# Split values in layer 1, later reads, loads and stores: one edit of a two-layer backbone kernel

## The chip, the core and the metric

The kernel runs on one core of one Trainium2 chip. The metric is the device time of one launch in microseconds (us). The engines are TensorE (PE; its weight loads are listed apart as PEld), VectorE (DVE), ScalarE (ACT), GpSimd (POOL) and SyncE (SP), which here only issues DMAs.

## What is computed

```python
for i in range(2):                                    # two layers; tokens 256 context + 1024 latent, D = 1024
    mod = silu(c) @ w_ada[i] + b_ada[i]               # six modulation vectors, for latent and for context
    h = modulate(rmsnorm(x, g_pre), sh1, sc1)
    p = h @ w_in[i]                                   # q (8 heads of 64), k, v (2 heads), u (512 columns)
    out = softmax(window and context scores, sink) @ v    # blocks of 128 queries, 3 + 2 blocks of keys
    four = fourier_mix(u, w_fourier[i])
    x_mid = x + g1 * rmsnorm(concat(out, four) @ w_out[i], g_post)
    hf = modulate(rmsnorm(x_mid, g_preffn), sh2, sc2)
    x = x_mid + g2 * rmsnorm((silu(hf @ w_gate[i]) * (hf @ w_up[i])) @ w_down[i], g_postffn)
    ...                                               # layer 0 does the same for the context tokens
```

Inputs and output are 32-bit. The large products are made of three cheaper ones each: an operand is split into a high part and the rest ("hi", "lo"), and hi·hi, lo·hi and hi·lo are added up in PSUM.

## The kernel before

The 1280 tokens lie in `X` (SBUF, features on partitions) in two blocks of 640 columns; in layer 1 the latent tokens alone, 512 and 512. A layer runs through these stages: input projection (`inproj`), attention (`attn`) with the rest of the projection, the Fourier mixing and the first block's output projection as filling work (`fill`), the second output projection, the FFN's up part (`ffn_up`, f16 products from sums of quarter matrices) and its down part (`ffn_down`).

**Order.** Stages are generators, and `mix` takes the next step from the one that has done the smallest share of its length; a scheduler then orders each engine's instructions by a model of their times. Each engine then runs its own list in that order, and so does SP: a DMA that has to wait, for a buffer or for its source, holds all DMAs behind it.

**Attention.** `Pair` (a class) does one unit: 128 queries, two heads. `score` makes the scores and their exponentials; `turn` transposes two key tiles of 128 (four transposes, L227) into a PSUM tile `tp` and ACT copies it to SBUF (`PT`, a ring of six, L231); `value` multiplies them by `V`. A unit has 5 key tiles, in the first and last query block 4, so 3 turns or 2; there are 32 units in layer 1. `value` packs: the product of an even key tile writes PSUM partitions 0 to 63, that of an odd one 64 to 127, both plain 32-bit (L244), and `finish` adds the halves. The score products are of another 32-bit type, `fp32r`; the profile shows both as f32.

**PSUM.** `ps` is a ring of four tiles that `tp`, `pv`, the narrow projections (`accn`), the Fourier products and the modulation share.

**Weights.** `weight` (L398 to L402) loads a 512 KB tile into `raw` (a ring of four), ACT casts it to hi, DVE makes lo. `ada` (L541, L570) makes layer 0's modulation with loads in the same ring, one load ahead of its products throughout the attention. `ahead` and `sums` make the weights of four FFN pairs early and store hi (ACT's queue, L471) and lo (SP's queue, L472) in DRAM.

**FFN down.** `hidden` issues the reads of hidden values that went to DRAM (L1198): 3 tiles of block 0, then all 11 of block 1, two reads each. `ffn_down` loads each w_down row in three pieces (L1211), scales them by hidden-tile factors (ACT L1216, DVE L1217) and multiplies (L1224).

**Between the layers.** The second block's post-norm (`postnorm`, L786 adds the residual) runs beside layer 1's first projections; with `share=True` every other add goes to POOL. Then `xstats` (squares, a sum by TensorE at L669 into `nps`, some DVE steps) and `spread` (L691, `rps`) give the norm that `scaled` (L714) uses.

```python
            mix((fill, FILL[l]), (self.attn(l, queries), ATT[l]), (work, 17), (early, 8 * AHEAD))
...
        for blk in range(2):
            for f in range(KEPT if blk == 0 else 0, NP):
                for e in range(2):
                    self.nc.sync.dma_start(places[blk][f][e], self.hs[blk, f, e, :, 0:w2])
```

## Time and profile before

| | us |
|---|---|
| median of three runs | 2496.72 (2495.13 to 2501.28) |
| the profiled execution | 2501.49 |
| its span, first to last instruction | 2499.7 |
| PE, DVE, ACT, POOL busy | 2377.2, 1658.1, 1347.8, 201.2 |
| mean granted clock of TensorE | 0.982 of full speed |

Busy time is counted per engine, and engines overlap, so it does not add up to the span. TensorE is busy for 95% of it; a granted clock below 1 means that it ran part of the time at 1.2 GHz in place of 2.4.

### The profile page before, as it was taken

The numbers are of one execution on the slowest core, as the hardware profiler recorded it, in microseconds if no ns is written. First come the engines' busy times: TensorE is split into PE (matmuls) and PEld (weight loads), VectorE is DVE, ScalarE is ACT, GpSimd is POOL, SyncE is SP. The second block draws the span as 40 slices with busy tenths as digits, with TensorE's granted clock in tenths as the row PEclk, the third lists the DMA queues.
The fourth block names the chain that finished last, engine by engine and source line by source line (L and its number), as shares of the span: only waits on it lengthen the run. The fifth ranks groups of instructions, "written<-read, shape, count | busy, mean of one in ns | idle before, by whom it ended". The sixth has DMA issues, their size and how long they took to land. (4 is left out here: it accounts for less than half of the span.)

```text
span 2499.7 us, 43891 instructions
## 1 busy us (share of the span) xinstructions
PE 2377.2 (95%) x17212; PEld 1856.0 (74%) x17212; DVE 1658.1 (66%) x3338; ACT 1347.8 (54%) x2587; POOL 201.2 (8%) x204
## 2 busy tenths in 40 slices
PE   7989989999999999998999989999989999999997
PEld 4877777797776666665777877877778888884586
DVE  5457676567837887777864595574677567765485
ACT  4476566657534455544654355576674456545473
POOL 0313110010000000000000043210100000000000
PEclk9999989999999999999999989999999999999998
DMA  8535423567654334559774231101496512237474
GB/s 303 188 112 176 154 94 119 195 226 280 209 180 139 124 129 161 159 193 365 271 246 145 94 119 39 35 18 51 172 341 221 169 60 85 77 107 243 131 251 130
DMA packets 157376, 406.83 MB, mean 163 GB/s; under 512 B 17488, under 2 KB 34288, under 8 KB 157168
## 3 DMA queue, kind: packets, MB, share of 16 engines
q1 hardware_dynamic: 147952, 389.33, 46.4%
q10 hardware_dynamic: 9216, 14.68, 1.6%
q8 instruction: 135, 2.21, 0.3%
q14 instruction: 73, 0.60, 0.1%
HBM read 339.19 MB, written 64.76 MB: 162 GB/s over the span
## 5 line engine op out<-in xcount | busy, mean ns | idle before, releaser
L1086 PE MATMUL p<-ffn,ww 128*128 128x320 f16 (+1 forms) x7392 | 923.4, 287 | 29.0 <-ACT ww L466 7.7
L1086 PEld LDWEIGHTS <-ww 128*128 128x128 f16 x7392 | 723.2, 98 | 226.1 <-issue 25.9
L1224 PEld LDWEIGHTS <-wd 128*128 128x128 f16 x3696 | 362.3, 98 | 167.1 <-ACT wd L1216 10.4
L1224 PE MATMUL acc<-hid,wd 128*128 128x320 f16 (+2 forms) x2544 | 335.7, 294 | 9.4 <-ACT wd L1216 9.1
L520 PE MATMUL accn<-arena,hi 128*128 128x320 f32 (+1 forms) x992 | 266.8, 336 | 4.6 <-ACT arena L231 2.3
L1217 DVE SCALAR_TENSOR_TENSOR wd<-raw,dn,wd 128x256 f16<-128x256 f32 x440 | 186.3, 481 | 126.2 <-ACT wd L1216 126.1
L1216 ACT ACTIVATE wd<-raw,dn 128x256 f16<-128x256 f32 x440 | 186.6, 496 | 134.7 <-PE acc L1224 78.1
L520 PE MATMUL acc<-arena,hi 128*128 128x320 f32 (+2 forms) x928 | 211.7, 333 | 3.5 <-ACT X L1040 2.5
L520 PEld LDWEIGHTS accn<-arena,hi 128*128 128x128 f32 x992 | 175.4, 191 | 25.7 <-issue 11.4
L1224 PE MATMUL acc<-X,wd 128*128 128x320 f16 (+1 forms) x1152 | 190.3, 326 | 0.7 <-ACT wd L1216 0.4
L520 PEld LDWEIGHTS acc<-arena,hi 128*128 128x128 f32 x928 | 156.7, 192 | 21.9 <-issue 4.6
L520 PE MATMUL accn<-arena,lo 128*128 128x320 f32 (+1 forms) x496 | 160.2, 326 | 0.0
L676 POOL TENSOR_TENSOR nr<-nm,mhalf 128x5 f32<-128x5 f32 (+2 forms) x17 | 19.9, 1169 | 1707.0 <-DVE nm L675 1670.9
L402 DVE TENSOR_TENSOR lo<-raw,hi 128x1024 fp32r<-128x1024 f32 x77 | 100.7, 1308 | 77.4 <-ACT hi L401 53.5
L216 DVE TENSOR_REDUCE ng<-score 128x1 f32<-128x641 f32 (+2 forms) x144 | 107.3, 747 | 63.6 <-PE score L209 62.0
L466 ACT ACTIVATE ww<-raw,sp 128x1024 f16<-128x1024 f32 x112 | 110.0, 1033 | 65.0 <-DVE raw L481 47.4
L231 ACT COPY arena<-tp 128x512 f32<-128x512 f32 (+1 forms) x184 | 96.7, 530 | 85.9 <-PE tp L227 84.2
L467 DVE SCALAR_TENSOR_TENSOR ww<-raw,sp,ww 128x1024 f16<-128x1024 f32 x112 | 125.8, 1147 | 25.0 <-ACT ww L466 24.8
L217 ACT ACTIVATE A<-score,ng 128x641 f32<-128x641 f32 (+2 forms) x144 | 106.5, 740 | 46.4 <-DVE ng L216 32.5
L401 ACT CAST hi<-raw 128x1024 fp32r<-128x1024 f32 x77 | 80.6, 1047 | 87.9 <-PE acc L520 37.1
L520 PE MATMUL acc<-arena,lo 128*128 128x320 f32 (+2 forms) x464 | 125.3, 329 | 0.0
L244 PE MATMUL pv<-arena 128*64 128x256 f32 x640 | 116.0, 407 | 2.5 <-ACT arena L231 2.5
(228 smaller groups left out, 3448.8 us busy)
## 6 DMA issues: line engine op xcount, KB each, us to landing
raw<-in_wdown SPq DMA_DIRECT2D x112, 512.0 KB, 4.8
ww<-wc SPq DMA_DIRECT2D x96, 512.0 KB, 4.5
raw<-in_wgate SPq DMA_DIRECT2D x60, 512.0 KB, 4.6
raw<-in_wup SPq DMA_DIRECT2D x60, 512.0 KB, 4.4
wm<-in_wada SPq DMA_DIRECT2D x96, 256.0 KB, 4.4
raw<-in_wdown SPq DMA_DIRECT2D x56, 384.0 KB, 4.6
raw<-in_win SPq DMA_DIRECT2D x40, 512.0 KB, 3.6
wada<-in_wada SPq DMA_DIRECT2D x39, 512.0 KB, 4.4
```

Of the source, the lines that this page charges most:

```text
L216: nc.vector.tensor_reduce(self.ng[:, hs], sv, axis=AX.X, op=ALU.max, negate=True)
L217: nc.scalar.activation(p, sv, AF.Exp, bias=self.ng[:, hs], accum_out=self.su[:, hs])
L231: nc.scalar.copy(pt, tp[:, 0:256 * n])
L244: nc.tensor.matmul(self.pv[HD * i:HD * i + HD, 0:256], net.V[:, self.kts[k], self.g, :], pt[:, 256 * i:256 * i + 256], start=(j == 0), sto ...
L402: nc.vector.tensor_tensor(lo[:, 0:w], raw[:, 0:w], hi[:, 0:w].bitcast(F32), op=ALU.subtract)
L466: nc.scalar.activation(hi, src, AF.Copy, scale=s)
L467: nc.vector.scalar_tensor_tensor(lo, src, s, hi, op0=ALU.mult, op1=ALU.subtract)
L520: self.nc.tensor.matmul(ps, wt[:, ks], xt[:, a:b], start=(k == 0 and i == 0), stop=(k == n - 1 and i == 2))
L1086: nc.tensor.matmul(ps, w[:, at:at + P], G[k // 2][:, k % 2, x, c, 0:h], start=(start and k + t == 0), stop=(k == KD // 2 - 1 and t == 2), ...
L1216: nc.scalar.activation(wt[:, 0, c], raw[:, c], AF.Copy, scale=r)
L1217: nc.vector.scalar_tensor_tensor(wt[:, 1, c], raw[:, c], r, wt[:, 0, c], op0=ALU.mult, op1=ALU.subtract)
L1224: nc.tensor.matmul(out, wt[:, e, k], xs[x][:, s, u:v], start=(f + s + i == 0), stop=(f == NP - 1 and s == 1 and i == 2))
```

## The change

In layer 1 (`whole` is false) `V` and the transposed exponentials are kept as hi and lo in `fp32r`; a value product is now 128 columns wide (V's hi beside its lo) and done twice, with the exponentials' hi and lo, for each key tile. DVE makes the lo parts. Two ring places serve one turn, so the six hold three turns. Layer 0 keeps the plain form.

Block 1's hidden reads become a third generator, `rest`, beside the first down products. A lo store of a made weight is issued at the next step of its generator and behind the latest load. `ada` has no standing load ahead: a unit loads its four tiles shortly before its products, then pauses for 1.7 steps; it no longer runs beside the first projection. Between the layers DVE does all residual adds, and the norm's steps are paced 8 to that projection, not 10.

```diff
@@ Pair.turn
-        pt = net.PT[net.npt % len(net.PT)][:, 0:256 * n]
-        net.npt += 1
+        parts = 1 if net.whole else 2
+        pt = [net.PT[(net.npt + e) % len(net.PT)][:, 0:256 * n] for e in range(parts)]
+        net.npt += parts
         with net.tc.high_priority(offset=AHEAD_OF):
-            nc.scalar.copy(pt, tp[:, 0:256 * n])
+            nc.scalar.copy(pt[0], tp[:, 0:256 * n])
+            if parts > 1:
+                nc.vector.tensor_tensor(pt[1], tp[:, 0:256 * n], pt[0].bitcast(F32), op=ALU.subtract)
@@ Pair.value
-            nc.tensor.matmul(self.pv[HD * i:HD * i + HD, 0:256], net.V[:, self.kts[k], self.g, :], pt[:, 256 * i:256 * i + 256],
-                             start=(j == 0), stop=(k + 2 >= len(self.kts)))
+            v, c = net.V[:, self.kts[k], self.g, :], slice(256 * i, 256 * i + 256)
+            if net.whole:
...
+            else:
+                for e in range(2):
+                    nc.tensor.matmul(self.pv[:, 0:256], v, pt[e][:, c], start=(k + e == 0), stop=(k == len(self.kts) - 1 and e == 1))
@@ sums
             if keep:
-                to = self.copy(l, i, j, self.WIDE[j])
-                nc.scalar.dma_start(to[:, 0], hi)
-                nc.sync.dma_start(to[:, 1], lo)
+                nc.scalar.dma_start(self.copy(l, i, j, self.WIDE[j])[:, 0], hi)
+                made.append((j, lo))
...
+        def store():
+            for j, lo in made:
+                with self.tc.issue_after(self.loaded.ins):
+                    nc.sync.dma_start(self.copy(l, i, j, self.WIDE[j])[:, 1], lo)
+            made.clear()
@@ ada
+            if not raws:
+                load()
+                yield 0.15
             for q in range(4):
-                load()
+                if ahead or q < 3:
+                    load()
...
-                yield 0.5
+                yield 0.5 if ahead else 0.15
...
-            yield 0.5
+            yield rest
@@ evac (values)
-                nc.scalar.copy(self.V[:, a // P + i0:a // P + i0 + n], src)
+                v = self.V[:, a // P + i0:a // P + i0 + n]
+                nc.scalar.copy(v[:, :, :, 0:HD], src)
+                if not self.whole:
+                    nc.vector.tensor_tensor(v[:, :, :, HD:P], src, v[:, :, :, 0:HD].bitcast(F32), op=ALU.subtract)
@@ hidden
+        def rest():
+            for f in range(NP):
+                read(1, f)
+                yield
+        for f in range(KEPT, NP):
+            read(0, f)
+        return places, rest()
@@ program
-        work = self.ada(0, range(4, 12), (1,), [])
-        next(work)
+        work = self.ada(0, range(4, 12), (), [], 1.7)
...
-                mix((self.inproj(l, 0, (3, 4, 5)), cost(3, KD, BW)), (side, 10), (part(work, 2), 1))
+                mix((self.inproj(l, 0, (3, 4, 5)), cost(3, KD, BW)), (side, 10))
             else:
-                mix((self.inproj(l, 0, (1, 0, 2, 3, 4, 5)), cost(6, KD, BW - C)), (side, 10))
+                mix((self.inproj(l, 0, (1, 0, 2, 3, 4, 5)), cost(6, KD, BW - C)), (side, 8))
...
-            mix((fill, FILL[l]), (self.attn(l, queries), ATT[l]), (work, 17), (early, 8 * AHEAD))
+            mix((fill, FILL[l]), (self.attn(l, queries), ATT[l]), (work, 20), (early, 8 * AHEAD))
...
-                mix(down(0, 0, w, first), (part(pre, 4 * AHEAD), 4 * AHEAD), (side, 32))
+                mix(down(0, 0, w, first), (part(pre, 4 * AHEAD), 4 * AHEAD), (side, 32), (rest, 14))
...
-                first, side = self.postnorm(l, 1, a1, b1, done, share=True), self.xstats(*B, "B")
+                first, side = self.postnorm(l, 1, a1, b1, done), self.xstats(*B, "B")
```

**The SP queue where layer 0's down products begin**, before, from the second piece of w_down on (`hid` are reads of hidden values, `wc` stores of lo, `raw<-in_wdown` pieces of w_down):

```order
298 L1211 DMA raw<-in_wdown 128x1024
299 L1198 DMA hid_11317<-hs 128x1280 x6
300 L1198 DMA hid_11318<-hs 128x1280 x4
301 L1137 DMA hs<-hid 128x1280 x2
302 L1198 DMA hid_11319<-hs 128x1280 x6
303 L1198 DMA hid_11317<-hs 128x1280
304 L1198 DMA hid_11319<-hs 128x1280
305 L1198 DMA hid_11317<-hs 128x1280
306 L1198 DMA hid_11319<-hs 128x1280
307 L1198 DMA hid_11320<-hs 128x1280 x6
308 L472 DMA wc<-wa 128x1024
309 L472 DMA wc<-wa 128x512
```

The third and fourth pieces follow as rows 310 and 311. The same stretch of the change:

```order
279 L1248 DMA raw<-in_wdown 128x1024
280 L1228 DMA hid_11318<-hs 128x1280 x6
281 L1228 DMA hid_11319<-hs 128x1280 x4
282 L1167 DMA hs<-hid 128x1280 x2
283 L1228 DMA hid_11320<-hs 128x1280 x6
284 L1228 DMA hid_11318<-hs 128x1280
285 L1228 DMA hid_11320<-hs 128x1280
286 L1228 DMA hid_11318<-hs 128x1280
287 L1248 DMA raw<-in_wdown 128x768
288 L1228 DMA hid_11320<-hs 128x1280
289 L1228 DMA hid_11321<-hs 128x1280 x2
290 L482 DMA wc<-wa 128x1024
```

The third piece moved ahead of seven reads and two stores; the fourth is row 293, behind one more store and three more reads.

**TensorE's list where layer 1 begins**, before (`acc` are products of the projection, `nps` and `rps` the norm's sum and spread); the transposes of the values stand 24 products ahead of `nps`:

```order
13829 L520 MATMUL acc<-arena_14484,lo 128x384
13830 L520 MATMUL acc<-arena_14484,hi 128x384
13831 L669 MATMUL nps<-cst,ssq 128x1 x5
13832 L691 MATMUL rps<-cst,nr 128x128 x5
13833 L520 MATMUL acc<-arena_14483,hi 128x384
```

In the change those transposes stand 34 products ahead of `nps` (row 13856), and these rows follow it:

```order
13857 L543 MATMUL acc<-arena_14484,lo 128x384
13858 L543 MATMUL acc<-arena_14484,hi 128x384
13859 L543 MATMUL acc<-arena_14485,hi 128x384
13860 L543 MATMUL acc<-arena_14485,lo 128x384
13861 L543 MATMUL acc<-arena_14485,hi 128x384 x2
13862 L543 MATMUL acc<-arena_14485,lo 128x384
13863 L543 MATMUL acc<-arena_14485,hi 128x384 x2
13864 L543 MATMUL acc<-arena_14485,lo 128x384
13865 L543 MATMUL acc<-arena_14485,hi 128x384 x2
13866 L543 MATMUL acc<-arena_14485,lo 128x384
13867 L543 MATMUL acc<-arena_14485,hi 128x384
13868 L718 MATMUL rps<-cst,nr 128x128 x5
```

So 24 products of 384 columns moved from behind `rps` to places ahead of it, 10 of them ahead of `nps`.

**A unit's value products on TensorE in layer 1**, before, all five key tiles of one unit together:

```order
14918 L209 LDWEIGHTS bf_101
14919 L209 MATMUL score<-sink,bf_101 128x1
14920 L244 MATMUL pv<-arena_14518 64x256 x5
14921 L252 MATMUL pv<-cst,pvl 128x128
14922 L227 MATMUL tp<-cst,A 128x128 x4
```

and in the change (L254; `PTX` is the sixth ring place, a tile of its own):

```order
15005 L254 MATMUL pv<-arena_14519 128x256
15006 L254 MATMUL pv<-PTX,arena_14519 128x256
15007 L254 MATMUL pv<-arena_14519 128x256
15008 L254 MATMUL pv<-PTX,arena_14519 128x256
15009 L254 MATMUL pv<-arena_14519 128x256 x5
15010 L227 MATMUL tp<-cst,A 128x128 x4
15011 L254 MATMUL pv<-arena_14519 128x256
15012 L261 MATMUL pv<-cst,pvl 128x128
```

Five products of 64 columns became ten of 128.

## Rows read from the trace of the kernel before

**Rows 1.** The page, busy us, share of the span, instructions.
```profile
PE 2377.2 (95%) x17212; PEld 1856.0 (74%) x17212; DVE 1658.1 (66%) x3338; ACT 1347.8 (54%) x2587; POOL 201.2 (8%) x204
```

**Rows 2.** Busy us by stretch: stretch, length, each engine, granted clock, DMA share, GB/s.
```profile
200.00:300.00 100.00, 99.02 (x677) 80.44 (x674) 73.14 (x139) 59.88 (x120) 28.51 (x30) 1.00 0.52 172
300.00:360.00 60.00, 51.47 (x338) 40.44 (x338) 42.75 (x90) 35.03 (x73) 12.22 (x14) 0.86 0.34 119
...
1440.00:1480.00 40.00, 28.51 (x153) 27.87 (x152) 35.04 (x49) 15.23 (x23) 15.36 (x13) 0.83 0.36 117
1500.00:1780.00 280.00, 275.71 (x1840) 216.88 (x1839) 157.62 (x354) 169.85 (x382) 51.95 (x60) 1.00 0.12 40
1640.00:1700.00 60.00, 58.12 (x430) 47.33 (x429) 43.90 (x106) 40.56 (x94) 9.71 (x14) 1.00 0.06 19
```

**Rows 3.** Timeline of PE in layer 1's attention: start, us, instruction.
```profile
1603.34 0.28 PE L202 MATMUL score<-arena,qs 128*128 128x256 f32 x1
1603.46 0.28 PE L203 MATMUL score<-arena,qs 128*128 128x256 f32 x1
...
1604.40 0.31 PE L520 MATMUL accn<-arena,lo 128*128 128x320 f32 x1
1604.55 0.31 PE L520 MATMUL accn<-arena,hi 128*128 128x320 f32 x1
1604.79 0.65 PE L244 MATMUL pv<-arena 128*64 128x256 f32 x4
1605.37 0.45 PE L200 MATMUL score<-arena,qs 128*128 128x384 f32 x1
...
1606.73 1.08 PE L244 MATMUL pv<-arena 128*64 128x256 f32 x6
```

**Rows 4.** Line 244, stretch 1400 to 1800: ns min/median/max, first and last start.
```profile
L244 PE MATMUL pv<-arena x304: 379/379/431, 1508.2 to 1772.3; 128*64 128x256 f32 x152
```

**Rows 5.** Line 912: VectorE's subtraction with one operand in PSUM.
```profile
L912 DVE TENSOR_TENSOR arena<-v,arena x16: 664/683/693, 316.2 to 1661.7; 128x512 fp32r<-128x512 f32 x16
```

**Rows 6.** Timeline of SP, PE and ACT where layer 0's down products begin.
```profile
1111.82 14.62 SPq L1198 DMA_DIRECT2D hid<-hs  x16
1126.54 2.25 SPq L472 DMA_DIRECT2D wc<-wa  x2
1129.12 1.16 SPq L1211 DMA_DIRECT2D raw<-in_wdown  x2
...
1135.03 1.30 ACT L1216 ACTIVATE wd<-raw,dn 128x256 f16<-128x256 f32 x3 [10.30 <-DMA raw<-in_wdown]
...
1135.59 7.96 PE L1224 MATMUL acc<-hid,wd 128*128 128x320 f16 x36 [9.06 <-ACT wd L1216]
```

**Rows 7.** Waits of PE, stretch 1440 to 1480: total us, times, longest.
```profile
PE rps L691 <- DVE nr L681: 5.2, 1, 5.2
PE vps L834 <- ACT vt L829: 3.8, 1, 3.8
PE nps L669 <- DVE ssq L663: 2.4, 1, 2.4
```

**Rows 8.** Timeline of DVE and POOL between the layers.
```profile
1431.34 10.42 DVE L714 SCALAR_TENSOR_TENSOR X<-X,scl,r 128x640 f32<-128x640 f32 x8
1435.37 2.00 POOL L786 TENSOR_TENSOR X<-res,X 128x640 f32<-128x640 f32 x1 [0.91 <-ACT ssq L659]
1466.26 6.46 DVE L714 SCALAR_TENSOR_TENSOR X<-X,scl,r 128x640 f32<-128x640 f32 x8 [2.21 <-ACT r L693]
```

**Rows 9.** Timeline of ACT and PE in layer 0's attention.
```profile
313.32 1.04 ACT L401 CAST hi<-raw 128x1024 fp32r<-128x1024 f32 x1 [2.59 <-DMA raw<-in_tabs]
317.28 0.69 PE L227 MATMUL tp<-cst,A 128*128 128x128 f32 x2 [3.77 <-ACT arena L231]
```

**Rows 10.** Waits of the SP queue, stretch 95 to 420: total us, times, longest.
```profile
SPq L472 <- DVE wa L467: 43.4, 13, 8.4
SPq L541 <- PE ada L570: 34.8, 6, 16.2
```

More of the change, by code (lines that the diff above doesn't have):

```diff
@@ L243, in value @@
             k = 2 * j + i
-            nc.tensor.matmul(self.pv[HD * i:HD * i + HD, 0:256], net.V[:, self.kts[k], self.g, :], pt[:, 256 * i:256 * i + 256],
-                             start=(j == 0), stop=(k + 2 >= len(self.kts)))
+            v, c = net.V[:, self.kts[k], self.g, :], slice(256 * i, 256 * i + 256)
+            if net.whole:
+                nc.tensor.matmul(self.pv[HD * i:HD * i + HD, 0:256], v, pt[0][:, c], start=(j == 0), stop=(k + 2 >= len(self.kts)))
+            else:
+                for e in range(2):
+                    nc.tensor.matmul(self.pv[:, 0:256], v, pt[e][:, c], start=(k + e == 0), stop=(k == len(self.kts) - 1 and e == 1))
     def finish(self):
@@ L271, in __init__ @@
         self.A = one.tile([P, 8 * BW + 4], F32, name="A")
+        self.PTX = one.tile([P, 512], F32R, name="PTX")
         self.turn_to(0)
@@ L346, in turn_to @@
     def turn_to(self, l):
-        self.H, (g, v) = self.arena[l % 2], self.new_arena(1 - l % 2, F32)
+        self.whole = l == 0
+        self.H, (g, v) = self.arena[l % 2], self.new_arena(1 - l % 2, F32 if self.whole else F32R)
         self.KHI = [g[:, T * i:T * i + T] for i in range(2)]
         self.KLO = [g[:, 2 * T + T * i:2 * T + T * i + T] for i in range(2)]
-        self.V = v[:, 0:T].rearrange("p (t g d) -> p t g d", g=2, d=HD)
-        self.PT = [v[:, T + 512 * i:T + 512 * i + 512] for i in range(6)]
+        n = T if self.whole else 2 * T
+        self.V = v[:, 0:n].rearrange("p (t g d) -> p t g d", t=T // P, g=2)
+        self.PT = [v[:, n + 512 * i:n + 512 * i + 512] for i in range(6 if self.whole else 5)]
+        if not self.whole:
+            self.PT.append(self.PTX[:])
     def halves(self, i, shape, types, name):
@@ L397, in weight @@
         raw = self.raw.tile([P, 1024], F32, tag="raw", name="raw")
-        nc.sync.dma_start(raw[:, 0:w], src)
+        self.loaded = nc.sync.dma_start(raw[:, 0:w], src)
         hi = self.w.tile([P, 1024], F32R, tag="w", name="hi")
@@ L441, in load @@
         for j in range(2):
-            self.nc.sync.dma_start(raw[j][:], self.io[("wgate", "wup")[i % 2]][l, i // 2 + NP * j])
+            self.loaded = self.nc.sync.dma_start(raw[j][:], self.io[("wgate", "wup")[i % 2]][l, i // 2 + NP * j])
         return raw
@@ L462, in sums @@
         s = self.sp[l][:, 0, i:i + 1].bitcast(F32)
+        made = []
+        def store():
[3 more added lines that the diff above has]
+            made.clear()
         def parts(j, src):
@@ L477, in sums @@
         yield
+        store()
         nc.vector.tensor_tensor(a22, a21, a22, op=ALU.add)
@@ L483, in sums @@
         yield
+        store()
         parts(3, raw[1][:])
         yield
+        store()
     def ahead(self, l):
@@ L526, in gemm, with ada @@
         yield t
-    def ada(self, l, units, ahead, spare):
+    def ada(self, l, units, ahead, spare, rest=0.5):
         nc = self.nc
@@ L835, in evac @@
                 src = p2[:, 0:P * n].rearrange("p (t g d) -> p t g d", g=2, d=HD)
-                nc.scalar.copy(self.V[:, a // P + i0:a // P + i0 + n], src)
+                v = self.V[:, a // P + i0:a // P + i0 + n]
+                nc.scalar.copy(v[:, :, :, 0:HD], src)
+                if not self.whole:
+                    nc.vector.tensor_tensor(v[:, :, :, HD:P], src, v[:, :, :, 0:HD].bitcast(F32), op=ALU.subtract)
         elif mt < 6:
@@ L1194, in hidden, with read @@
                   + [[far[i // 4][:, i % 4, e, 0:w2] for e in range(2)] for i in range(KEPT)]]
-        for blk in range(2):
-            for f in range(KEPT if blk == 0 else 0, NP):
-                for e in range(2):
-                    self.nc.sync.dma_start(places[blk][f][e], self.hs[blk, f, e, :, 0:w2])
-        return places
+        def read(blk, f):
+            for e in range(2):
+                self.nc.sync.dma_start(places[blk][f][e], self.hs[blk, f, e, :, 0:w2])
+        def rest():
[5 more added lines that the diff above has]
+        return places, rest()
     def ffn_down(self, l, blk, places, c0, c1, dst):
@@ L1318, in program @@
             mix((up, one * (44 - 4 * AHEAD)), (mod(0, 1), 64), (iter(()) if last else self.norms(l + 1), 2 * AHEAD))
-            places = self.hidden(l, blocks)
+            places, rest = self.hidden(l, blocks)
             down = lambda blk, c0, c1, dst: (self.ffn_down(l, blk, places, c0, c1, dst), cost(KD, KH_, c1 - c0))
@@ L1331, in program @@
                 run(self.operands(l + 1, *A))
-                first, side = self.postnorm(l, 1, a1, b1, done, share=True), self.xstats(*B, "B")
+                first, side = self.postnorm(l, 1, a1, b1, done), self.xstats(*B, "B")
             else:
-                mix(down(0, 0, w, first))
+                mix(down(0, 0, w, first), (rest, 14))
                 self.down_scale(1)
```

## The prediction

> **What bounds the kernel now.** I read the page's busy line first: TensorE is busy for 95% of the span [rows 1], so the time falls only where TensorE gets less to do or waits less. Then I cut the span into stretches [rows 2]. The reader is to see three kinds: layer 0's attention from 200 to 300 us, where TensorE is 99% busy although VectorE is 73% busy; two gaps with a fallen clock (300 to 360: 8.5 us idle, granted clock 0.86; 1440 to 1480: 11.5 us idle, 0.83); and layer 1's attention (1500 to 1780), full at 275.7 of 280 us at full clock. In the last, only fewer or shorter products help; in the gaps, an earlier transfer or a shorter chain. For each place touched I then read what ended the wait: the timeline, the waits of TensorE, and those of the SP queue.
>
> **Value products.** The 32 units make 24 x 3 + 8 x 2 = 88 turns in 1508 to 1772 us, and their 152 products are 304 records [rows 4]. A stretch of one turn takes 1605.37 - 1604.79 = 0.58 us until the next product starts; the record of two turns is 1.08 - 0.65 = 0.43 longer [rows 3]. So a turn holds TensorE for 0.43 us, and each stretch adds 0.15. The product ahead of it also holds it longer, 0.24 in place of 0.15 [rows 3]. With 74 such stretches in the timeline, layer 1 pays 88 x 0.43 + 74 x (0.15 + 0.09) = 37.8 + 17.8 = 55.6 us. After the change there are 152 x 2 = 304 products of 256 columns in `fp32r`. The nearest row is a score product, same type and width, with 0.12 us from one to the next [rows 3]; such products stand among the projection's without the extra times. That is 304 x 0.12 = 36.5 us, so 19 us less. The other end is that the switching times stay: 37.8 - 36.5 = 1.3 us less. I take 19, since the score rows are the same kind of instruction among the same neighbours.
>
> These rows show what the packing gave: a turn with one key tile costs as much as a turn with two. The Trainium skill, TensorEngine Tiling (Array Packing), section Theoretical Speedup, promises up to twofold for a dimension of 64 or less, and the change gives that up; the trace agrees that two packed products share one product's time. By that rule alone the 1.3 us end would hold; it is a rival below.
>
> **VectorE pays for it.** 64 turns get a subtraction of 512 columns at 0.69 us and 24 one of 256, whose price no row here gives; between 0.35 and 0.69 I take 0.4, as most of the cost grows with the columns. Together 44 + 10 = 54 us [rows 5]. VectorE's share from 1500 to 1780 goes from 157.6 of 280 to 212 of 261, so 81%, which rows 2 bear (73% beside a TensorE that is 99% busy). In the Fourier part, 1640 to 1700, it goes from 43.9 of 60 to some 55 of 56, because TensorE needs less there too. It has no cover left, so I add 6 us; the bounds are 0 and what the worst stretch of layer 0 would make of it (rival 2). What would be late is the lo part: `tp` is released after ACT and DVE, and three more tiles later TensorE wants the place again.
>
> **Down, layer 0.** SP issues 16 reads in 14.62 us (0.91 each), then two stores until 1129.12, then the third piece of w_down; ACT has it at 1135.03, and TensorE had waited 9.06 us [rows 6]. In the change seven reads and two stores no longer stand ahead of that piece: 7 x 0.91 + (1129.12 - 1126.54) = 9.0 us earlier, so the wait almost goes. But six of these reads and the stores now stand ahead of the fourth piece: 6 x 0.91 + 2.6 = 8.0 us behind the third, while the 36 products of the third take 36 x 0.133 = 4.8 us at full clock; a new wait of 3.2. The 36 took 7.96 at the lowered clock, so 3.1 were lost to it; I count half back. Together 9.0 - 3.2 + 1.5 = 7 us; bounds 0 and 12.2. In layer 1 the same edit saves nothing, since TensorE did not wait there.
>
> **Start of layer 1.** TensorE waits 3.8 + 2.4 + 5.2 us [rows 7]: for values that ACT copies behind squares that wait for DVE's residual adds, for the sum, and for the norm. Two edits meet here. VectorE's eight products took 10.42 us while POOL's adds of 2.00 each ran beside them, against 6.46 without [rows 8]: 4 us less, and four adds more at 0.8, with two splits of V behind them. The chain is some 2 us shorter, and its first adds are done before ACT wants them, so the first wait goes (3.8). Of the 24 products moved ahead of `rps`, 10 fill the time to `nps` and 14 that behind it, at 0.17 us each (4 us). The later waits partly stay, since the sum still ends on VectorE behind the splits: 2 + 4 = 6 us in all. Bounds: 0, and 11.5 plus the 3 that the clock of 0.83 costs.
>
> **Layer 0's attention.** The modulation's loads and the lo stores hold the SP queue: stores waited 43.4 us in 13 waits for VectorE, loads 34.8 in six for the modulation's products [rows 10]. Little of it reaches TensorE: the DFT table comes 2.59 us late to ACT, and TensorE waits 3.77 [rows 9], then runs slowly for a while [rows 2]. Both edits clear that queue. In place of one load ahead come bursts, in the same four places, whose products follow sooner; so not all is gain. I take 4 us, that one wait; bounds: all of the 17 us that 300 to 360 lost (8.5 idle and 0.14 x 60 of clock), and a loss of 30 (rival 3). The pacing numbers and the loads' record cost nothing by themselves.
>
> **Sum.** -19 + 6 - 7 - 6 - 4 = -30 us against the profiled execution's own 2501.5 (span 2499.7, with 1.8 around it): 2471.5. That execution was 4.8 above the median of the three runs, so for the median 2496.7 I forecast **2467 us**.
>
> **Rivals.**
> 1. The switching times stay, or come back with the transposes, which are still plain 32-bit. Then 18 us of the 19 are lost: 2485. Against it stand the score rows; for it, half of the stretches stand next to transposes.
> 2. VectorE becomes the bound of layer 1's attention. If its 261 us lose what 300 to 360 lost, 17 us in 60, that is 74 us, 68 more than counted: 2535, slower. For it: in both stretches VectorE is over 70% busy with ACT's and TensorE's work between its own. Against: 200 to 300 has the same share and loses 1 us. It decides the sign from 36 us of stalls on, or 8 us in 60.
> 3. The bursts come late. If each of the eight modulation units stalls TensorE once like the table load, 8 x 3.77 = 30 us replace the 4 gained: 2501, no gain.
> 4. The waits at the two joints only move: the reads still stand ahead of the third piece, and the norm is still late. Then 13 us are missing: 2480.
>
> **Chances and range.** Forecast 0.58, rival 1 0.12, rival 2 0.09, rival 3 0.08, rival 4 0.13. A measurement of this kernel tells about 0.3% (7.5 us) from no change. Forecast and rivals 1 and 4 are faster (0.83, of which I give 0.02 to no change), rival 3 is split, rival 2 slower: faster 0.81, same 0.09, slower 0.10. The range reaches down by the open gains (6 of VectorE, 5 down, 8 at layer 1's start, half of layer 0's 13), not all at once: 2442; up past rivals 4 and 1 to 2492.
>
> **What would show it.** Value products of 0.12 us each without a long neighbour, and the stretch of layer 1's attention some 13 us shorter; VectorE near 80% there, with TensorE's waits naming DVE subtractions in the Fourier part. At the down products a wait near 0, and one of 3 us behind the third piece. At layer 1's start no wait for the values, and two shorter ones. In layer 0's attention no wait of ACT for the table. I am wrong if the stretch of layer 1's attention gets longer, if TensorE waits for modulation loads, or if the value products take over 0.15 us each.

## The result, and the profile after

The changed kernel takes 2476.44 us (median of 5, 2472.94 to 2483.38) where the kernel before takes 2495.13 on the same chip: ratio 0.9928, 95% interval 0.9903 to 0.9952, 18 us faster. I forecast 2467 (2442 to 2492), 30 us faster. Sign and range hold; two fifths of the gain are missing. The profiled execution took 2482.05 us, its span is 2480.2: 19.5 less than before.

The engines' line of the page after, against [rows 1]:

```profile
PE 2353.2 (95%) x17212; PEld 1867.4 (75%) x17212; DVE 1695.2 (68%) x3434; ACT 1347.7 (54%) x2587; POOL 190.5 (8%) x200
```

The stretches after, columns as in [rows 2]; the last two start earlier, as the stages do:

```profile
300.00:360.00 60.00, 55.44 (x401) 43.31 (x399) 50.88 (x113) 42.05 (x87) 12.49 (x14) 0.97 0.48 160
1435.00:1475.00 40.00, 29.02 (x167) 28.12 (x166) 37.05 (x53) 17.48 (x26) 14.47 (x13) 0.91 0.41 145
1490.00:1762.00 272.00, 260.01 (x1870) 242.00 (x1869) 202.57 (x454) 170.50 (x385) 53.58 (x64) 0.99 0.14 45
```

The gap at 300 to 360 us is half closed (clock 0.97 for 0.86). The gap at layer 1's start is as long as before at a better clock. In layer 1's attention VectorE is at 74%, and TensorE, full before, is now idle for 12 us.

Value products in TensorE's timeline, answering [rows 3]:

```profile
1583.76 0.52 PE L254 MATMUL pv<-arena 128*128 128x256 f32 x3
1584.12 0.34 PE L200 MATMUL score<-arena,qs 128*128 128x384 f32 x1
...
1584.86 0.36 PE L254 MATMUL pv<-arena 128*128 128x256 f32 x1
1585.06 0.31 PE L543 MATMUL accn<-arena,hi 128*128 128x320 f32 x1
```

Three products hold TensorE for 0.36 us, 0.12 each, as forecast; one behind the scores' small 16-bit products holds it 0.20 (1584.86 to 1585.06).

Layer 0's down products, answering [rows 6]:

```profile
1107.46 7.35 SPq L1228 DMA_DIRECT2D hid<-hs  x9
1116.20 0.33 SPq L1248 DMA_DIRECT2D raw<-in_wdown  x1
...
1119.23 1.15 ACT L487 ACTIVATE wa<-raw,sp 128x1024 f16<-128x1024 f32 x1
1126.98 0.33 ACTq L491 DMA_DIRECT2D wc<-wa  x1
1127.40 1.30 ACT L1253 ACTIVATE wd<-raw,dn 128x256 f16<-128x256 f32 x3 [7.03 <-DMA hid<-hs]
1134.64 0.79 ACT L1267 ACTIVATE A<-acc,dback 128x640 f32<-128x640 f32 x1 [5.93 <-PE acc L1261]
...
1136.11 1.69 ACT L1253 ACTIVATE wd<-raw,dn 128x256 f16<-128x256 f32 x4
...
1127.97 6.63 PE L1261 MATMUL acc<-hid,wd 128*128 128x320 f16 x36 [5.80 <-ACT wd L1253]
1136.65 5.63 PE L1261 MATMUL acc<-X,wd 128*128 128x320 f16 x26 [2.05 <-ACT wd L1253]
```

The third piece is issued early, and it lands early. The view of DMAs gives its size and the time from issue to landing, before and after:

```profile
raw<-in_wdown SPq DMA_DIRECT2D x1, 384.0 KB, 5.8
```

```profile
raw<-in_wdown SPq DMA_DIRECT2D x1, 384.0 KB, 5.9
```

So it was there at 1122.1, but ACT takes it up at 1127.40, 11.2 us after its issue, where it took 1135.03 - 1129.12 = 5.9 before [rows 6]. In between stands a store of a made weight's hi (L491) in ACT's own list. Its tile was ready at 1120.38, yet it was issued at 1126.98: by the semaphores in the trace it waited for the read that SP issued at 1121.14 and that landed at 1126.90. (The timeline's "<-DMA hid<-hs" names a read as well, not the piece.) The fourth piece landed at 1129.76; ACT scales it at 1136.11, behind an eviction (L1267), which waits for TensorE's products, and a square. So waits of 5.80 and 2.05 stand where one of 9.06 stood, and both end in ACT's list.

TensorE's waits between the layers (1415 to 1500), answering [rows 7]:

```profile
PE rps L718 <- DVE nr L708: 7.9, 1, 7.9
PE vps L861 <- ACT vt L856: 3.8, 2, 2.7
...
PE nps L696 <- DVE ssq L690: 0.4, 1, 0.4
```

The wait for values, which was to go, went from 3.8 to 2.7 us; the other 1.1 lies behind it and stood there before too. The sum comes earlier and the norm does not: counted from the norm sum before it (the second half's, in the down products), `nps` starts after 33.0 us in place of 36.0, `rps` after 44.7 in place of 42.5. VectorE's timeline shows what lies between; the sum's products end at 1451.2, and the norm's first step (`nm`) stands in VectorE's list behind low parts of the keys (L852) and of a weight (L416):

```profile
1450.00 1.65 DVE L852 SCALAR_TENSOR_TENSOR arena<-kr,arena 64x640 fp32r<-64x640 f32 x2
...
1452.75 2.86 DVE L852 SCALAR_TENSOR_TENSOR arena<-kr,arena 64x640 fp32r<-64x640 f32 x2
1455.64 1.22 DVE L416 TENSOR_TENSOR lo<-raw,hi 128x1024 fp32r<-128x1024 f32 x1
1456.79 0.16 DVE L702 TENSOR_SCALAR nm<-nps 128x5 f32<-128x5 f32 x1
```

In layer 0's attention (165 to 600) the wait for the table is gone from TensorE's list and is 1.2 us in ACT's. But TensorE waits for modulation loads, which I had named as a sign of being wrong; it is small:

```profile
PE ada L597 <- DMA wada<-in_wada: 3.4, 2, 2.4
```

**Stage by stage.** The landmarks are in TensorE's timeline: the first products of `nps` for layer 0's FFN norm, `dsum` at the end of FFN up, `nps` after each half of the down products, the last `vps`, the next `nps` (end of attention), the first `dsum` of layer 1. Each number is the distance of two starts, in us, rounded; TensorE's last products start 238.5 to 239.0 behind the last column in all.

| profiled execution | start to FFN norm | FFN up, layer 0 | down, block 0 | down, block 1 | joint to layer 1's values | attention, layer 1 | on to end of FFN up, layer 1 |
|---|---|---|---|---|---|---|---|
| before | 647.9 | 462.9 | 177.7 | 133.3 | 84.1 | 273.6 | 468.0 |
| after | 639.7 | 466.7 | 177.2 | 133.3 | 82.2 | 261.0 | 468.2 |
| after, repeated | 638.0 | 467.0 | 177.6 | 133.3 | 82.2 | 261.0 | 467.1 |
| split alone | 642.5 | 460.9 | 175.6 | 133.3 | 86.4 | 261.0 | 461.9 |
| no split | 636.5 | 462.9 | 175.7 | 133.3 | 82.4 | 273.8 | 468.8 |
| old reads | 639.4 | 462.8 | 175.7 | 133.3 | 82.0 | 259.5 | 460.9 |
| late reads | 636.5 | 466.5 | 175.9 | 133.3 | 81.5 | 262.3 | 461.4 |
| late reads, late modulation | 637.1 | 463.7 | 165.6 | 133.7 | 81.6 | 261.0 | 463.5 |
| the same, pace 10 | 638.4 | 461.7 | 165.6 | 140.4 | 82.0 | 262.4 | 460.9 |
| late modulation alone | 636.9 | 466.3 | 176.9 | 137.8 | 81.8 | 261.0 | 467.7 |
| old modulation loads | 645.4 | 464.3 | 177.3 | 133.3 | 81.6 | 261.0 | 461.9 |
| old stores | 636.8 | 470.7 | 176.8 | 133.3 | 81.8 | 260.9 | 461.8 |
| old joint | 638.5 | 462.5 | 177.3 | 133.3 | 85.3 | 260.9 | 462.1 |
| no low part | 639.5 | 466.8 | 177.1 | 133.3 | 82.4 | 251.7 | 462.3 |

The 19.5 us of the span, with rounded terms: start -8.2, FFN up +3.8, down -0.5, joint -1.9, attention -12.6, the rest -0.2.

### The profile page after: what moved, and what is told of

Same layout as the page of the kernel before. It is cut to its first block, busy times and chain, and to the rows that moved or that the text cites. A ratio compares the mean times of both kernels' runs of the same rounds, so it can differ in the third digit from the quotient of the medians.

```text
span 2480.2 us, 44040 instructions
## 1 busy us (share of the span) xinstructions
PE 2353.2 (95%) x17212; PEld 1867.4 (75%) x17212; DVE 1695.2 (68%) x3434; ACT 1347.7 (54%) x2587; POOL 190.5 (8%) x200
## 5 line engine op out<-in xcount | busy, mean ns | idle before, releaser
L543 PE MATMUL accn<-arena,hi 128*128 128x320 f32 (+1 forms) x992 | 260.9, 332 | 1.7 <-DVE PTX L234 0.7
L1253 ACT ACTIVATE wd<-raw,dn 128x256 f16<-128x256 f32 x440 | 187.2, 496 | 130.7 <-PE acc L1261 81.5
L416 DVE TENSOR_TENSOR lo<-raw,hi 128x1024 fp32r<-128x1024 f32 x77 | 99.2, 1289 | 66.6 <-ACT hi L415 50.0
L217 ACT ACTIVATE A<-score,ng 128x641 f32<-128x641 f32 (+2 forms) x144 | 106.6, 741 | 34.9 <-DVE ng L216 19.5
L464 ACT ACTIVATE junk<-raw 128x1024 bf16<-128x1024 f32 x88 | 92.4, 1052 | 40.5 <-DMA raw<-in_wup 21.1
L690 DVE TENSOR_TENSOR ssq<-ssq,sq 128x640 f32<-128x640 f32 (+2 forms) x119 | 89.8, 755 | 31.5 <-ACT sq L689 28.6
```

Of the source, the lines that this page charges most:

```text
L217: nc.scalar.activation(p, sv, AF.Exp, bias=self.ng[:, hs], accum_out=self.su[:, hs])
L416: nc.vector.tensor_tensor(lo[:, 0:w], raw[:, 0:w], hi[:, 0:w].bitcast(F32), op=ALU.subtract)
L464: self.nc.scalar.activation(junk[:], raw[j][:], AF.Square, accum_out=self.ss[:, j, i:i + 1])
L543: self.nc.tensor.matmul(ps, wt[:, ks], xt[:, a:b], start=(k == 0 and i == 0), stop=(k == n - 1 and i == 2))
L690: nc.vector.tensor_tensor(s[:, 0:w], s[:, 0:w], t[:, 0:w], op=ALU.add)
L1253: nc.scalar.activation(wt[:, 0, c], raw[:, c], AF.Copy, scale=r)
```

## Experiments

**The split, alone and left out.** On the kernel before, the change's hunks in `turn`, `value`, `evac` and `turn_to`; then the change without them.

```diff
+            nc.vector.tensor_tensor(pt[1], tp[:, 0:256 * n], pt[0].bitcast(F32), op=ALU.subtract)
...
-            nc.tensor.matmul(self.pv[HD * i:HD * i + HD, 0:256], net.V[:, self.kts[k], self.g, :], pt[:, 256 * i:256 * i + 256],
+                    nc.tensor.matmul(self.pv[:, 0:256], v, pt[e][:, c], start=(k + e == 0), stop=(k == len(self.kts) - 1 and e == 1))
```

> The kernel before with the split of the values in layer 1 as its only change. Theory (304 narrow-type products of 0.12 us take the place of packed plain 32-bit products that held TensorE for 55.6 us, and VectorE's waits give 6 of the 19 back): the stretch of layer 1's attention gets about 13 us shorter, and the whole kernel 12 to 14 us faster than before, about 2482; the rest of the program stays where it was, within 2 us. Rival (most of the gain of this stretch comes from the other edits, which clear queues and pacing): under 6 us faster, and layer 1's attention is shortened by less than half of the 12.6 us that the whole change showed.

> The changed kernel with the values of layer 1 kept whole again (packed plain 32-bit products as before), all other edits kept. Theory (the split alone is worth 13 us): about 2489, some 6 us faster than before, and layer 1's attention as long as before. Rival (the other edits are worth as much as the 18 us in all): about 2478. That the two single effects add up would show in this run's loss against the changed kernel being as large as the gain of the kernel with the split alone.

Measured: 2477.25 us alone, ratio 0.9916 (0.9891 to 0.9940); 2492.48 without it, 0.9973 (0.9959 to 0.9986). The attention is as expected: 261.0 wherever the values are split, 273.6 and 273.8 where not. The whole is not: alone, the split seems worth 21 us, as much as the whole change. The table shows why: of the 26 us between the two profiled executions 12.6 come from the attention, 2.3 are lost at the joint, and some 16 come from stretches that this edit does not touch, 6.1 of them in layer 1's FFN up. Left out of the change, the split costs nothing at the joint: 82.4 us against 82.2.

**Reads as before, and reads held back.**

```diff
         def rest():
+            yield
+            yield
             for f in range(NP):
-                read(1, f)
+                with self.tc.issue_after(self.loaded.ins):
+                    read(1, f)
                 yield
...
-(rest, 14)
+(rest, 16)
```

> The changed kernel with the second block's down input read all at once again, as before; the other edits are kept. Theory A, by which I forecast (the third piece of the down weights lands a fixed 6 us after its issue, so the order of the issues decides): the wait at the start of layer 0's down products grows by the 7 us forecast, about 2483. Theory B (the piece lands when the bytes that were queued ahead of it have been moved; the reads put behind it still share the same DMA engines): the start of the down products is as long as in the changed kernel within 1.5 us, and so is the whole.

> The changed kernel with the second block's reads held back further: none of the 22 stands ahead of the third piece of the down weights (13 did in the changed kernel), and each pair is issued behind the latest load of down weights. Theory B (bytes queued ahead decide): the third piece lands within 6 us of its issue, the waits of 5.80 and 2.05 us at the start of the down products go, and with them part of the lowered clock: 6 to 9 us faster than the changed kernel, about 2469. Theory A (a fixed landing time; only the place of the issue counts): the third piece is issued 7 reads later than it could be in the changed kernel already, and pulling it ahead of 13 more reads of 0.9 us each removes at most the 5.8 us wait, about 2471, but its time from issue to landing stays at 11 us. Rival C (something else than the DMA sets these waits, such as ACT's or DVE's queue): no change, 2476.

Measured: old reads 2469.88 us, 0.9878 (0.9855 to 0.9900); late reads 2468.29, 0.9869 (0.9844 to 0.9894). With all reads at once the first down products take 175.7 us, not 7 more. The third piece lands 5.8 us after its issue there, 5.9 in the change, 3.7 with late reads. So the landing time of some 6 us in theory A holds for the change; what fails is the step from the landing to the wait. With the reads as before ACT takes the piece 0.1 us after it landed, in the change 5.3 us after, behind its store. From the end of FFN up TensorE goes on after 23.7 us with the old reads and 21.6 in the change, and the wait of 2.05 takes that back. Theory B names the right total for a reason that the trace does not show: at both waits of the change it was ACT's list, rival C. With late reads the two first waits are gone, and two others stand further on, as TensorE's timeline of that kernel shows:

```profile
1105.78 12.94 PE L1264 MATMUL acc<-X,wd 128*128 128x320 f16 x94 [0.18 <-DVE wd L1257]
...
1139.72 5.31 PE L1264 MATMUL acc<-hid,wd 128*128 128x320 f16 x36 [3.05 <-ACT wd L1256]
1167.13 3.11 PE L1264 MATMUL acc<-X,wd 128*128 128x320 f16 x11 [4.17 <-ACT wd L1256]
```

3.05 + 4.17 = 7.2 us, where the change has 5.80 + 2.05 = 7.9 and old reads 8.0. ACT stands at stores again, issued at 1138.79 and 1165.52; the piece behind the first had landed at 1135.54:

```profile
1138.79 0.33 ACTq L491 DMA_DIRECT2D wc<-wa  x1
1139.16 1.31 ACT L1256 ACTIVATE wd<-raw,dn 128x256 f16<-128x256 f32 x3 [4.04 <-DMA hid<-hs]
```

So holding the reads back removes the first waits and not the sum. Both kernels are faster than the change, but not there: the 7 us lie in layer 1's FFN up again.

**The change once more.**

> The changed kernel once more, unaltered, on the chip of the runs that come with it. From layer 1's first post-norm sum to the end of its FFN up part, which no edit touches, three kernels with one TensorE order took 468.0 to 468.8 us and three with two other orders 460.9 to 461.9. Theory O (the scheduler's order in this stretch, re-rolled by edits elsewhere, costs 7 us): 468 again, and the whole at 2476 again, 6 to 9 us above the kernel with late reads. Rival N (variation from execution to execution): the stretch comes out anywhere from 461 to 469, and the whole nearer to 2469. Layer 0's FFN up part (466.6 in the changed kernel, 460.9 to 462.9 in four others of the same TensorE order, 466.5 in one) should differ from 466.6 if that is mere variation.

Measured: 2480.53 us against 2501.96 before, 0.9921 (0.9904 to 0.9938); the stretch took 467.1: theory O. Of the 14 profiled executions the five with TensorE's order of before (before, after twice, no split, late modulation alone) take 467.1 to 468.8 us from attention to the end of FFN up, the eight with two other orders 460.9 to 462.3, the one with a fourth 463.5. The two sum rows of this stretch, first of the change, then of the kernel with old reads:

```profile
sum 468.20, PE 453.04 PEld 397.95 DVE 325.28 ACT 252.10 POOL 10.87; mean PE 453.04 PEld 397.95 DVE 325.28 ACT 252.10 POOL 10.87
```

```profile
sum 460.90, PE 451.87 PEld 398.09 DVE 327.03 ACT 251.45 POOL 10.69; mean PE 451.87 PEld 398.09 DVE 327.03 ACT 251.45 POOL 10.69
```

TensorE is idle for 15.2 us in the one and 9.0 in the other, with the same work. That its order makes the difference rests on these groups; no run changed the order alone. Layer 0's FFN up came out at 467.0 again, where mere variation should have made it differ from 466.7. The other kernels spread from 460.9 to 470.7 there, with one order of TensorE in all. So the 3.8 us which the changed kernel lost there may be its own; what makes the spread was not settled.

**Modulation loads moved to the second down products, with late reads and without.**

```diff
-                pre, side = self.ahead(l + 1), mod(2)
-                mix(down(0, 0, w, first), (part(pre, 4 * AHEAD), 4 * AHEAD), (side, 32), (rest, 16))
+                pre, m2 = self.ahead(l + 1), mod(2)
+                mix(down(0, 0, w, first), (part(pre, 4 * AHEAD), 4 * AHEAD), (rest, 16))
...
-                mix(down(1, 0, w, lambda m: self.X[:, m, a1:b1]), (side, 32), (pre, 8 * AHEAD))
+                mix(down(1, 0, w, lambda m: self.X[:, m, a1:b1]), (side, 32), (pre, 8 * AHEAD), (m2, 36))
```

> The kernel with late reads, and the 32 modulation loads (8.4 MB) that ran beside layer 0's first down products moved to the second ones, where the DMA engines are busy for 0.22 to 0.69 of the time. Theory B' (the first 90 us of the down products are bound by the bytes that the DMA engines have to move, so waits of 7 to 9 us in all only change place with the order of the reads): with 8.4 MB less, some 20 us of transfers at 400 GB/s, the 7.2 us of waits go, the first down products take 169 us instead of 176, and nothing is paid behind them: 2461 to 2463. Rival (the waits come from the order in SP's queue, not from bytes): waits of 5 us or more stay there, 2466 to 2469. Rival 2 (the modulation's work on VectorE is late for the norm between the layers): the start of layer 1 gets longer by as much as is gained.

> The changed kernel with the 32 modulation loads moved to layer 0's second down products, its hidden reads as in the changed kernel. It tells whether the 10 us that the kernel with late reads and late modulation loads gained there need both. Theory (bytes queued ahead of the third piece set the first wait, the bytes of the next 90 us the later ones): the first wait of about 6 us stays, the 2 us behind it go, and the first down products take 173 to 175 us against 177 and 165.6. Rival (only the sum of bytes counts): 166 to 168. The order in layer 1's FFN up part is the slow one of the changed kernel, 467 to 468 us.

Measured: with late reads 2463.43 us, 0.9865 (0.9840 to 0.9890); without 2483.60, 0.9935 (0.9919 to 0.9951). The stretches 1103 to 1193 of the kernel with late reads, then of the one with both:

```profile
1103.00:1133.00 30.00, 29.47 (x219) 20.81 (x217) 27.25 (x64) 15.57 (x27) 0.00 (x0) 1.00 0.86 306
1133.00:1163.00 30.00, 26.84 (x196) 18.70 (x193) 22.98 (x48) 11.49 (x20) 0.00 (x0) 1.00 1.02 383
1163.00:1193.00 30.00, 25.87 (x172) 17.71 (x173) 22.78 (x52) 15.56 (x30) 0.00 (x0) 0.89 0.98 360
```

```profile
1103.00:1133.00 30.00, 29.78 (x219) 21.28 (x220) 26.62 (x53) 18.22 (x32) 0.00 (x0) 1.00 0.92 314
1133.00:1163.00 30.00, 30.00 (x223) 21.61 (x221) 22.29 (x43) 19.10 (x38) 0.00 (x0) 1.00 0.99 359
1163.00:1193.00 30.00, 30.00 (x223) 21.60 (x222) 22.87 (x41) 16.85 (x33) 0.00 (x0) 1.00 0.97 355
```

With both no wait over 0.4 us is left: 165.6 us, 10.3 less than late reads alone. Loads moved alone leave 5.50 and 2.05 us of waits, so my 173 to 175 was wrong too (176.9). The first is again a store in ACT's list, issued at 1123.38; the third piece had landed at 1120.27. Either edit alone only hands the wait on. Whether it is fewer bytes or another order in ACT's list that frees the stores with both, no run parts.

**Pace 10 on top of that, and the old joint.**

```diff
-                mix((self.inproj(l, 0, (1, 0, 2, 3, 4, 5)), cost(6, KD, BW - C)), (side, 8))
+                mix((self.inproj(l, 0, (1, 0, 2, 3, 4, 5)), cost(6, KD, BW - C)), (side, 10))
...
-                first, side = self.postnorm(l, 1, a1, b1, done), self.xstats(*B, "B")
+                first, side = self.postnorm(l, 1, a1, b1, done, share=True), self.xstats(*B, "B")
```

The kernel with pace 10 has the first hunk, on late reads and late modulation; the old joint has both, on the change.

> The kernel with late reads and late modulation loads, and the norm's steps between the layers paced 10 again, not 8; all adds stay with VectorE. This parts the joint's two edits. Theory (what counts is that VectorE's products no longer run beside GpSimd's adds, forecast at 4 us): 82 us for the joint, as with both. Rival (the pace counts): 84 to 86. The order of layer 1's FFN up part is that of the kernel with late reads, 461 us where the kernel with late modulation loads took 463.5, so the whole would be 2 us below that one by the theory, 0 to 2 above it by the rival.

> The changed kernel with the joint between the layers as before: every other residual add on GpSimd, and the norm's steps paced 10 to the projection. From the second norm sum of layer 0's down products to the last values of layer 1 the kernel before took 84.1 us, the one with the split alone 86.4, all kernels with the new joint 81.4 to 82.4. Theory (the new joint is worth 4 us beside the split, whose two extra VectorE steps cost 2): 86 us here. Rival (these 4 us come from another edit): 82. TensorE's order in layer 1's FFN up part is that of the kernel with the split alone, so that part should take 462 us, not 467 to 468; the whole would then be within 3 us of the changed kernel.

Measured: pace 10 2465.24 us, 0.9862 (0.9837 to 0.9888); old joint 2476.72, 0.9900 (0.9885 to 0.9916). The joint takes 82.0 us with pace 10 and 85.3 with GpSimd's adds: for the sum the adds count and the pace does not. The pace only trades one part of the joint for the other, up to `rps` and on to the last values:

| | to `rps` | on |
|---|---|---|
| before | 42.5 | 41.6 |
| after | 44.7 | 37.5 |
| late reads, late modulation | 44.3 | 37.3 |
| the same, pace 10 | 40.5 | 41.6 |
| old joint | 43.7 | 41.6 |

VectorE's eight products of the first norm, in the change and in the old joint:

```profile
1426.56 6.45 DVE L741 SCALAR_TENSOR_TENSOR X<-X,scl,r 128x640 f32<-128x640 f32 x8
```

```profile
1421.23 10.41 DVE L741 SCALAR_TENSOR_TENSOR X<-X,scl,r 128x640 f32<-128x640 f32 x8
```

Pace 10 missed its total for another reason: its second down products took 140.4 us. VectorE's and TensorE's timelines there:

```profile
1282.49 0.75 DVE L674 CUSTOM_DVE_ANT_0 wm<-wm,c,bada 128x512 f32<-128x512 f32 x1 [2.58 <-DMA wm<-in_wada]
...
1283.77 0.17 DVE L708 TENSOR_TENSOR nr<-nr,ne 128x5 f32<-128x5 f32 x1
1284.08 1.30 PE L718 MATMUL rps<-cst,nr 128*128 128x128 f32 x5 [4.14 <-DVE nr L708]
```

A modulation load that had moved there holds VectorE ahead of the norm's last steps. In the kernel with both edits the same wait on `rps` was 0.22, in late modulation alone 2.62. So moving the loads has a price at this place, which a start behind the norm may avoid; that was not tried.

**Modulation loads as before, and stores as before**: the hunks `ada` and `program`, and the hunk `sums`, undone.

```diff
-        work = self.ada(0, range(4, 12), (), [], 1.7)
+        work = self.ada(0, range(4, 12), (1,), [])
+        next(work)
```

```diff
-                made.append((j, lo))
+                nc.sync.dma_start(self.copy(l, i, j, self.WIDE[j])[:, 1], lo)
```

> The changed kernel with the modulation's loads as before: one load ahead all through layer 0's attention, two steps beside the first projection. Up to the FFN norm of layer 0 the kernel before took 647.9 us and the one with the split alone 642.5, the four with all other edits 636.5 to 639.9. Theory (the bursts, not the stores, carry this gain): this comes out at 642 to 648 there, with the first norm at 77 us instead of 73.5. Rival (the stores carry it): 636 to 640. The order in layer 1's FFN up part is that of the kernel with the split alone here, so that 462 us are expected for that stretch instead of 468, and the whole would be 2474 to 2478 by the theory, 2469 by the rival.

> The changed kernel with the lo stores of made weights issued at once again, as before. Theory (the bursts carry the gain in layer 0's attention, the stores little): 636 to 640 us up to the FFN norm of layer 0, as in the changed kernel. Rival (the stores carry it): 642 to 648, with waits of TensorE for the table or for modulation loads behind held stores. The order in layer 1's FFN up part is again that of the kernel with the split alone, so 462 us are expected for that stretch, and the whole would be 2469 by the theory, 2474 to 2478 by the rival.

Measured: old modulation loads 2481.14 us, 0.9921 (0.9906 to 0.9937), 645.4 up to the FFN norm; old stores 2472.49, 0.9888 (0.9870 to 0.9907), 636.8. The modulation's loads carry this gain, 5.7 to 8.9 us against the kernels that have the new ones. Its size is less certain than that: the split alone, with the old loads too, takes 642.5. Putting the stores off gives nothing that can be seen, though undone they wait 63.4 us for VectorE in the SP queue (14 waits). Part of the gain comes ahead of the attention: with the old loads TensorE waits 2.7 us for the first norm of block B, in the change 0.8:

```profile
PE rps L714 <- DVE nr L704: 2.7, 1, 2.7
```

```profile
PE rps L718 <- DVE nr L708: 0.8, 1, 0.8
```

**No low part.** Both products of a key tile use the high part of the exponentials.

```diff
-                nc.vector.tensor_tensor(pt[1], tp[:, 0:256 * n], pt[0].bitcast(F32), op=ALU.subtract)
+                pt[1] = pt[0]
```

> The changed kernel without VectorE's subtractions that make the low part of the transposed exponentials in layer 1: both products of a key tile use the high part, so the low part of the exponentials is left out of the result; the number of products is the same. Theory (VectorE's work costs the 6 us that I forecast): layer 1's attention takes 255 us, not 261. Rival (VectorE had cover after all, and something else takes the rest): 260 to 261. TensorE's order in the FFN up part is that of the kernel with late reads (461 us), so the whole falls by another 7 us for that reason alone: about 2464 by the theory, 2470 by the rival.

Measured: 2464.89 us, 0.9852 (0.9834 to 0.9869). The attention takes 251.7 us in place of 261.0: VectorE's subtractions cost 9.3, 3 more than forecast. TensorE's waits in the change (1499 to 1760) that are not in this kernel:

```profile
PE score L200 <- ACT A L217: 2.5, 3, 1.4
PE tp L227 <- DVE PTX L234: 1.9, 1, 1.9
...
PE pq L1005 <- DVE arena L234: 1.0, 1, 1.0
PE accn L543 <- DVE PTX L234: 0.7, 1, 0.7
PE pv L254 <- DVE arena L234: 0.5, 1, 0.5
```

## Why the prediction was right, and where its steps failed

| term | forecast | measured | from |
|---|---|---|---|
| value products | -19 | -22 | 273.6 to 251.7, no low part |
| VectorE | +6 | +9.3 | 251.7 to 261.0 |
| down, layer 0 | -7 | -0.5 (old reads are no slower) | 175.7 against 177.2 and 177.6 |
| start of layer 1 | -6 | -1.9 | 84.1 to 82.2 |
| layer 0 up to the FFN norm | -4 | -5.7 to -8.9 | old modulation loads |

**Right: the value products decide.** The attention's net gain of 13 came out at 12.6. That is in part luck: both terms behind it were too small by 3, and the misses cancel. Summed from each record's start to the next one's, waits taken off, the value products held TensorE for 52.6 us before, and for 40.6 without the low part (43.0 in the change): 12 of the 22. The other 10 lie in the neighbours, which I had charged at one place only: the transposes hold it 27.9 us in place of 32.9, the narrow projection 107.7 for 111.2. VectorE's price of 9.3 is rival 2's mechanism at an eighth of its 74 us: its 0.683 and 0.416 us subtractions match my 0.69 and 0.4, and 4.5 us of the waits name them. Over the whole stretch VectorE is at 74%, but in the Fourier part at 54.1 of 60 us, as forecast, and there TensorE is idle for 6.9 us where it was for 1.9 (before, then after):

```profile
1630.00:1690.00 60.00, 58.12 (x440) 47.35 (x439) 45.46 (x113) 42.82 (x102) 11.88 (x16) 1.00 0.06 19
```

```profile
1613.00:1673.00 60.00, 53.10 (x426) 48.92 (x425) 54.10 (x128) 41.16 (x96) 12.06 (x16) 1.00 0.06 19
```

VectorE's subtractions, grouped by form (1499 to 1760):

```profile
L234 DVE TENSOR_TENSOR arena<-tp,arena 128x512 fp32r<-128x512 f32 x33 | 22.6, 683 | 12.9 <-ACT arena L232 12.8
...
L234 DVE TENSOR_TENSOR arena<-tp,arena 128x256 fp32r<-128x256 f32 x24 | 10.0, 416 | 2.5 <-ACT arena L232 2.4
```

**Wrong: "9.0 us earlier, so the wait almost goes".** Counted from the end of FFN up the issue came 8.5 us earlier and the landing 8.4, near my 9.0: that step holds. The next one, from the landing to the end of TensorE's wait, I put at nothing. There ACT's list held the piece for 5.3 us behind a store that waited for a later read to land, and the fourth piece behind an eviction, for a new wait of 2.05. Why the store waited: in this trace the DMAs of SP and ACT take turns on eight semaphores, and each is issued only after the one eight before it has landed. So a DMA that an engine issues can hold that engine's own work. This is read from the trace; a kernel with the store behind the scaling was not run. Rival 4 (the waits only move) was the true one at this place, but not for its reason. The DMA engines were full before and after, as the rows of the 30 us from the end of FFN up show (before, then after):

```profile
1110.80:1140.80 30.00, 20.40 (x132) 13.24 (x130) 21.05 (x49) 11.46 (x20) 0.00 (x0) 0.84 1.03 396
```

```profile
1106.40:1136.40 30.00, 21.86 (x148) 14.34 (x145) 16.93 (x40) 10.50 (x18) 0.00 (x0) 0.89 1.04 401
```

The Trainium skill, Perfetto Trace Analysis, section Roofline, gives about 435 GB/s as the bound of one core's 16 DMA engines; the 401 measured lie under it, and no row shown here reaches it.

**Wrong: 2 + 4 at layer 1's start.** The 2 came. "4 us less" on VectorE was right (6.45 for 10.41), and with pace 10 the norm is there after 40.5 us where it took 42.5. The 4 did not come. The products moved ahead of `rps` take 4.1 us off what follows it (41.6 to 37.5), and the norm comes about as much later (40.5 with pace 10, 44.3 with 8), since its steps stand in VectorE's list behind the work that these products bring. I had filled TensorE's wait and left out that VectorE works for the fill. The splits of V, which I had put behind the products without a price, cost 2.3 us beside the old joint (84.1 to 86.4, split alone) and nothing beside the new one (82.4 without, 82.2 with).

**Undersized: layer 0.** I took one wait of 4 us. The modulation's edit gives up to twice that, a part of it ahead of the attention, since no modulation runs beside the first projection any more; I had that edit in the text and gave it no price. Rival 3 (the bursts come late) is there at a tenth of its 30 us: the 3.4 us of waits for modulation loads.

**Not foreseen: other stretches.** Layer 1's FFN up is 5 to 8 us longer in the order that before and after share. It cancels in the result and hides in every experiment whose edit happens to re-roll it.

The best kernel of the study is the change with late reads and late modulation loads: 2463.43 us, ratio 0.9865, 34 us faster than before by the ratio; on one chip with the repeated change, 17 faster than that. Pace 10 on top is no different (0.9862).

## What to carry to other kernels

A transfer that lands earlier helps only when the engine that takes it is free to: read what stands ahead in that engine's own list, a store that it issues included, and follow the wait to its end, since reordering alone moved it here. The same holds for products that fill a wait: count the work they bring to the engine that ends it. Where a scheduler sets the order, compare experiments stage by stage: an edit can re-roll a stretch far away and win or lose there more than it is worth. And price a slow kind of instruction by its neighbours too, which it slows as well.

## What the runs showed of the hardware that I had not expected

- The same load of down weights landed 5.8 us after its issue before and 5.9 in the change, at DMA shares of 1.03 and 1.04. ACT used it 0.1 us later in the one and 5.3 in the other, where a store in ACT's list had to wait for a read to land.
- VectorE's product with two operands in SBUF takes 10.41 / 8 = 1.30 us beside GpSimd's adds and 0.81 without. The Trainium skill, SBUF — State Buffer, section SBUF: two separate sides, says that a VectorE instruction with two operands in SBUF and a GpSimd one that reads SBUF exclude each other for a whole instruction. The trace agrees in direction; the loss of 3.96 us is less than the 6.09 of the three adds that ran within those products.
- A wait of 4.14 us in otherwise full TensorE work cost 7 us: in the 20 us behind it the granted clock was 0.88, with 132 products where the other kernel did 149. First pace 10, then late reads and late modulation:

```profile
1285.00:1305.00 20.00, 20.00 (x132) 13.72 (x131) 18.74 (x40) 6.02 (x13) 0.00 (x0) 0.88 0.72 240
```

```profile
1286.00:1306.00 20.00, 20.00 (x149) 14.41 (x148) 18.69 (x40) 5.66 (x13) 0.00 (x0) 1.00 0.88 295
```

- One order of TensorE in layer 0's FFN up gave 460.9 to 470.7 us in 14 profiled executions, at granted clocks of 0.99 to 1.00; the changed kernel gave 466.7 and 467.0. What makes these 10 us was not settled.
